# Adding the experts' returned rows by accumulating DMAs, and moving seven p @ ple_proj steps into the first expert pair

## The chip, the cores and the metric

The kernel runs on one core of a Trainium2 chip. The metric is the device time of one execution in microseconds; the median of three runs is given. A further execution was recorded by the hardware profiler, and all rows of the trace come from that one.

## The reference

One decoder layer over 512 tokens of width 1024, in float32. Three head groups (gated linear attention, stick-breaking attention, pooling) are mixed and added to x; call the sum h. Then comes a mixture of experts: for each token one of four groups, and two of the eight experts in it. Then a gated per-layer embedding, and a last norm:

```python
h = h + mix @ w_out
t = rmsnorm(h, norm2_g)                    # routed: top-1 group, top-2 experts of 32
y = sum over the two experts e of combine[e] * (silu(t @ w_gate[e]) * (t @ w_up[e])) @ w_down[e]
h = h + y
gate = sigmoid(rmsnorm(h, ple_norm_g) @ ple_gate_w + ple_gate_b)
h = h + gate * (p @ ple_proj_w)
return rmsnorm(h, final_norm_g)
```

## The kernel before

Tokens lie in four tiles of 128 (t = 0 to 3), kept in SBUF as h1[t], 128 x 1024. After the mixers `ffn` runs three stages.

Routing. For each tile `route_in` transposes the two halves of h1[t] on TensorE, copies them out on ScalarE (L759) and sums the squares there (L761); `logits` multiplies the halves by the router's matrix (L766); `route` is a generator of small VectorE steps, which first scales the tile's rows and writes them to a table in DRAM (tnd, L776) and then finds the group and the two experts (L780 to L813); `position` counts each expert's tokens before the tile (L820, L821), which gives a slot for each token. `one_hot` and `slot_sums` turn this into a list of tokens for a pair of experts, and `fetch` (L917) gathers their rows from tnd by an indirect DMA on Pool into xg. In the last part of this stage `ple(n)` issues the next n of sixteen steps of p @ ple_proj_w (L718, copied out by L720 into eo); step by step they are spread between the routing of tiles 2 and 3 by the tuple PLE, and fifteen stand ahead of gather_T(0, 0) and one behind it. PE and SP run in the order in which the program is written, VectorE too in this block.

Experts. Sixteen pairs (i = 0 to 15) run one after the other. `gather_T` transposes the pair's token rows (L941, scaled into xT by L942), `gate_up` multiplies them by the gate and up matrices in eight steps k with two experts each (L953), `down` by the down matrix (L985). Behind each k the function made by `between(i)` prepares a later pair. The result of a pair goes by an indirect DMA on Pool (L998) to its tokens' rows of yd in DRAM, which has one block of 512 rows for the first expert and one for the second. Pair 15 alone doesn't go through yd: `scatter` adds it by a matmul with a one-hot (L1006) and a VectorE add into h1 (L1008).

Weights come as 1 MB slabs, six a pair, by `load_units` on SP (L689). Slots are handed round in a ring: `free` puts a slot at its end, `load_units` loads into each slot that the ring has, and waits for the slot's last reader. Each load also waits for the load three before it (AHEAD). Slabs are taken in the order 0, 3, 1, 4, 2, 5 of a pair: the first two are used by k = 0 to 3 of `gate_up`, the next two by k = 4 to 7, the last two by `down`. The matrix ple_proj_w (pW) holds one slot of the ring, freed ahead of the first pair.

Tail. From pair 14 on VectorE and ScalarE too run in the written order. On SP stand the loads of ple_gate_w (`gate_load`, four of 1 MB), two rows and the four reads of yd (`load_y`, both returns of a tile in 1 MB). `add_y(t)` adds the two returns to h1[t] on VectorE (L1090). `split_gate(k)` splits a row block of the gate matrix into two parts (ScalarE L1019, VectorE L1022). `turn(t, hf)` transposes h1[t] (L1140) and splits it, `last(t)` multiplies it by the gate matrix (L1161) and `finish` makes the output. The adds and scatter of tile t + 1 stand in the middle of tile t's products.

Of the kernel before, what the change touches and what calls it, by code (L numbers as in the profile page):

```python
# [17 lines left out]
P = 128  # L18
S = 512
# [10 lines left out]
PLE = (2, 1, 2, 3, 1, 2)  # L30
# [581 lines left out]
def ffn(ctx, tc, A, K, mixh, mixl, out, dbg, stage):  # L612
# [99 lines left out]
    def ple_steps():  # L712

        for j in range(8):
            t, hf = j // 2, j % 2
            p = ps("pe", "pe")
            for k in range(2):
                PE.matmul(p, pT[:, k * S + t * P:k * S + (t + 1) * P], pW[:, k, hf * 512:hf * 512 + 512], start=(k == 0), stop=(k == 1))  # L718
                if k:
                    e = SC.activation(eo[t // 2][:, t % 2, hf * 512:hf * 512 + 512], p, AF.Copy)  # L720
                yield e if k else None
# [27 lines left out]
    def route_in(t, hf):  # L749

        if hf == 0:
            rt_in[t] = small("ms2", 2), {}, ps("pl", "po")
        ms2, hT, pl = rt_in[t]
        hs = slice(hf * 512, hf * 512 + 512)
        p = zt("xt")
        for k in range(4):
            PE.transpose(p[:, k * P:(k + 1) * P], h1[t][:, (4 * hf + k) * P:(4 * hf + k + 1) * P], ident)
        hT[hf] = xt_half(hf)
        SC.activation(hT[hf].rearrange("p k n -> p (k n)"), p, AF.Copy)  # L759
        junk = mw.tile([P, 512], BF, name="junk", tag="hidT")  # L760
        SC.activation(junk, h1[t][:, hs], AF.Square, accum_out=ms2[:, hf:hf + 1])  # L761
# [62 lines left out]
    def weights(t, g8, e8, id2, c0):  # L824
# [7 lines left out]
        SC.activation(ed, d, AF.Exp)  # L832
# [192 lines left out]
    with tc.manual_schedule(engines={mybir.EngineType.DVE}):  # L1025
        position(1)
        steps = [route(t) for t in (NT - 2, NT - 1)]
        run(steps[0], 7)
        ple(PLE[0])
        logits(NT - 1, 0)  # L1030
        ple(PLE[1])
        logits(NT - 1, 1)
        for t in (0, 1):
            one_hot(0, t)
        load_units(1)
        while run(steps[0], 1):
            run(steps[1], 1)
        ple(PLE[2])
# [3 lines left out]
        ple(PLE[3])  # L1042
        one_hot(0, 2)
        position(NT - 1)
        ple(PLE[4])
# [5 lines left out]
        ple(PLE[5])  # L1051
# [6 lines left out]
    ple(15 - sum(PLE))  # L1058
    for hf in range(2):
        gather_T(0, hf)  # L1060
    done = ple(1)
    with tc.issue_after(done.ins):
        SC.preload_act_table_set("silu_and_others")
    free(pW)
# [4 lines left out]
    def between(i):  # L1069

        def go(k):
            if k == (0 if i else 3) and i + 2 < 16:
                slots_of(i + 2)
            if k == 4 and i < 2:
                for t in range(NT):
                    one_hot(i, t)
            if k == (2 if i > 1 else 6):
                slot_weights(i)
            if k == 5 and i + 1 < 16:
                gather_T(i + 1, 0)  # L1080
            if i == 15 and k == 5:
                onehot_T(i)
        return go

    ys = []

    def add_y(t):

        for r in range(2):
            V.tensor_tensor(h1[t], h1[t], ys[t][:, r], ALU.add)  # L1090

    def load_y(t):
        ys.append(unit(F32, [P, 2, D]))
        nc.sync.dma_start(ys[t], yd.rearrange("(r n) d -> n r d", r=2)[t * P:(t + 1) * P])

    ends = ExitStack()
    for i in range(16):
# [3 lines left out]
        free(*(slab[6 * i + n] for n in (0, 3, 1, 4)))  # L1101
        if i == 15:
            break
# [5 lines left out]
        if i == 14:  # L1109
            gate_load(0)  # L1110
            load_y(0)
            for j in range(1, 4):
                gate_load(j)
            rows = mix.tile([P, 2, D], F32, name="rows", tag="m0")
            nc.sync.dma_start(rows[:, 0], bcast(A["ple_gate_b"]))
            for t in range(1, NT):
                load_y(t)
# [16 lines left out]
    def turn(t, hf):  # L1134

        if hf == 0:
            hT[t] = unit(F32R, [P, 2, D], slot_of[id(ys[t])][0])
# [63 lines left out]
    def sums(t):  # L1201
        add_y(t)
        for hf in range(2):
            scatter(2 * t + hf)
# [7 lines left out]
    def behind_down(n):  # L1212
        if n == 0:
            add_y(0)
        if n == 1:
            split_gate(0)
# [4 lines left out]
    split_gate(1)  # L1221
# [180 lines left out]
```

## Time and profile before

| | us |
|---|---|
| median of 3 runs | 562.84 |
| lowest, highest | 561.83, 564.35 |
| the profiled execution | 564.24 |
| its span, first to last instruction | 562.5 |
| TensorE busy (share of the span) | 515.2 (92%) |
| VectorE busy | 274.3 (49%) |
| ScalarE busy | 210.2 (37%) |
| Pool busy | 88.2 (16%) |

The span falls into the mixers (to about 197 us), the out projection with the routing (to about 249 us), the expert pairs (to about 484 us) and the tail. Busy shares are averages over stages with different limits. The profile's page gives the transfers' busy share in 40 equal slices of 14.06 us; queue q1 is that of SP, q0 the software queue of Pool. A chain of waits follows the last instruction back, at each step to what released it.

### The profile page before, as it was taken

How to read it: one execution, taken by the hardware profiler on the slowest of the kernel's cores; microseconds unless marked ns; L12 is line 12 of the kernel's file. 1: busy time of each engine (PE TensorE's matmuls, PEld its weight loads, DVE VectorE, ACT ScalarE, POOL GpSimd, SP SyncE). 2: the span in 40 equal slices, each digit the busy share in tenths (PEclk: the TensorE clock that was granted, in tenths of full speed). 3: DMA queues.
4: the chain of work that ended last, by engine and by line, in shares of the span. 5: the costliest groups of instructions: out<-in, count | busy, mean ns of one | idle time of the engine just before them, and what ended most of it. 6: DMA issues, size and time to landing. Idle time of an engine off the chain costs nothing.

```text
span 562.5 us, 7377 instructions
## 1 busy us (share of the span) xinstructions
PE 515.2 (92%) x2629; PEld 311.8 (55%) x2629; DVE 274.3 (49%) x729; ACT 210.2 (37%) x435; POOL 88.2 (16%) x125
## 2 busy tenths in 40 slices
PE   8999999999999999999999999998889888678992
PEld 5798886877997788743333333332322323247782
DVE  6662957756746664674422222222212101597774
ACT  7466665746757444441111111111111011364442
POOL 3300111221009400121111111111100100010000
PEclk9899999999999999999999999999999999899997
DMA  8882222300439669769999999999999999960111
GB/s 312 269 314 59 56 76 70 89 26 2 130 131 420 245 264 419 282 222 372 395 416 413 392 392 373 363 408 388 403 418 421 416 395 421 410 257 37 38 38 43
DMA packets 35787, 148.98 MB, mean 265 GB/s; under 512 B 6665, under 2 KB 13705, under 8 KB 22306
## 3 DMA queue, kind: packets, MB, share of 16 engines
q1 hardware_dynamic: 30562, 139.29, 64.2%
q0 software_dynamic: 4464, 8.11, 3.9%
q10 hardware_dynamic: 720, 1.05, 0.5%
q8 instruction: 23, 0.38, 0.3%
q14 instruction: 18, 0.15, 0.1%
HBM read 140.14 MB, written 16.25 MB: 278 GB/s over the span
## 4 chain that ended last, share of the span: by engine, by line
PE 62%; DMA 20%; DVE 8%; ACT 6%; issue 2%; POOL 1%; SPq 0%; DVEq 0%; ACTq 0%; POOLq 0%
DMA unit<-in_w_exp_dram 16%; PE gu L953 11%; PE pj L232 9%; PE po L78 8%; PE dn L985 6%; PE pj L255 5%; PE z L255 4%; PE pg L1161 3%; PE pe L718 2%; PE z L309 2%; PE po L331 2%; DMA yd<-big,idy 2%; DVE h L1090 2%; PE pl L766 1%; PE xt L941 1%
## 5 line engine op out<-in xcount | busy, mean ns | idle before, releaser
L953 PE MATMUL gu<-unit,xT 128*64 128x512 f32 x512 | 129.8, 601 | 6.2 <-DMA unit<-in_w_exp_dram 6.2
L953 PEld LDWEIGHTS gu<-unit,xT 128*64 128x64 f32 x512 | 36.5, 136 | 71.9 <-issue 55.4
L985 PE MATMUL dn<-unit,hidT 128*64 128x512 f32 x256 | 59.1, 598 | 7.6 <-ACT hidT L976 7.6
L942 DVE TENSOR_TENSOR xT<-xt,g2c 128x512 f32<-128x512 f32 x32 | 22.0, 688 | 66.4 <-PE xt L941 66.4
L958 ACT ACTIVATE sg<-gu 128x256 f32<-128x256 f32 x16 | 6.1, 384 | 126.0 <-PE gu L953 126.0
L232 PE MATMUL pj<-xh,wp 128*128 128x512 f32 x176 | 52.1, 403 | 0.2 <-ACT wp L67 0.2
L1161 PE MATMUL pg<-unit 128*128 128x512 f32 (+1 forms) x216 | 48.2, 378 | 1.2 <-DVE unit L1022 1.2
L1161 PEld LDWEIGHTS pg<-unit 128*128 128x128 f32 x216 | 37.2, 191 | 10.5 <-DVE unit L1022 3.2
L998 POOL DMA_INDIRECT yd<-big,idy x15 | 15.1, 1009 | 173.3 <-ACT big L989 173.3
L985 PEld LDWEIGHTS dn<-unit,hidT 128*64 128x64 f32 x256 | 18.1, 136 | 37.9 <-issue 25.3
L904 DVE COPY SL<-sl 128x10 f32<-128x10 f32 (+1 forms) x18 | 3.0, 168 | 72.7 <-PE sl L903 72.7
L232 PEld LDWEIGHTS pj<-xh,wp 128*128 128x128 f32 x176 | 33.2, 192 | 8.3 <-ACT wp L67 1.1
L989 ACT ACTIVATE big<-dn 128x512 f32<-128x512 f32 x30 | 17.9, 597 | 48.2 <-PE dn L985 48.2
L68 DVE TENSOR_TENSOR wp<-wraw,wp 128x768 fp32r<-128x768 f32 (+2 forms) x28 | 25.8, 928 | 15.3 <-ACT wp L67 15.1
L67 ACT ACTIVATE wp<-wraw 128x768 fp32r<-128x768 f32 (+2 forms) x28 | 22.8, 816 | 21.9 <-PE pj L232 9.8
L232 PE MATMUL pj<-xl,wp 128*128 128x512 f32 x88 | 30.0, 408 | 0.0
L941 PEld LDWEIGHTS xt<-ident,xg 128*128 128x128 f32 x128 | 13.5, 140 | 24.9 <-issue 24.6
L78 PE MATMUL po<-wo,mx 128*128 128x512 f32 x96 | 25.7, 408 | 0.0
L255 PE MATMUL pj<-wp,xh 128*128 128x384 f32 x96 | 24.8, 351 | 0.0
L78 PE MATMUL po<-unit,mx 128*128 128x512 f32 x96 | 23.8, 399 | 0.0
L941 PE MATMUL xt<-ident,xg 128*128 128x128 f32 x128 | 20.7, 286 | 0.0
L917 POOL DMA_INDIRECT xg<-tnd,idx x16 | 16.4, 1027 | 23.0 <-issue 13.1
(293 smaller groups left out, 847.5 us busy)
## 6 DMA issues: line engine op xcount, KB each, us to landing
unit<-in_w_exp_dram SPq DMA_DIRECT2D x96, 1024.0 KB, 8.3
wraw<-in_w_in_dram SPq DMA_DIRECT2D x20, 384.0 KB, 3.5
yd<-zero SPq DMA_DIRECT2D x4, 1024.0 KB, 8.6
unit<-in_ple_gate_w_dram SPq DMA_DIRECT2D x4, 1024.0 KB, 11.0
unit<-yd SPq DMA_DIRECT2D x4, 1024.0 KB, 16.1
wraw<-in_w_out_dram SPq DMA_DIRECT2D x8, 256.0 KB, 3.0
h<-in_x_dram SPq DMA_DIRECT2D x4, 512.0 KB, 5.3
unit<-in_w_out_dram SPq DMA_DIRECT2D x4, 512.0 KB, 9.6
```

The costliest lines, as they stand in the source:

```text
L67: nc.scalar.activation(h, src, AF.Copy)
L68: nc.vector.tensor_tensor(l, src, h.bitcast(F32), ALU.subtract)
L78: nc.tensor.matmul(p, a[k][:, ts_], K["wo"][k][:, b, hs], start=(n == 0), stop=(n == 3 * len(ks) - 1))
L232: PE.matmul(q, a[:, i * P:(i + 1) * P], b[k], start=(n == 0), stop=(n == 3 * KC - 1))
L255: PE.matmul(p[t][:, :W_IN[j]], a[k][:, t * P:(t + 1) * P], b, start=(n == 0), stop=(n == 3 * KC - 1))
L917: G.indirect_dma_start(out=xg[i % 2], out_offset=None, in_=tnd, in_offset=bass.IndirectOffsetOnAxis(ap=idx[:, i:i + 1], axis=0), bounds_ch ...
L941: PE.transpose(p[:, k * P:(k + 1) * P], xg[i % 2][:, (4 * hf + k) * P:(4 * hf + k + 1) * P], ident)
L942: V.tensor_tensor(xTs[i, hf], p.rearrange("p (a b) -> p a b", a=4), g2c[:, 4 * hf:4 * hf + 4, None].to_broadcast([P, 4, P]), ALU.mult)
L953: PE.matmul(gu[64 * e:64 * e + 64], xTs[i, k // 4][:, k % 4, 64 * e:64 * e + 64], w[e][k // 4][:, 512 * (k % 4):512 * (k % 4) + 512], star ...
L985: PE.matmul(dn[64 * e:64 * e + 64], hT[:, f, 64 * e:64 * e + 64], w[e][2][:, 1024 * f + 512 * hf:1024 * f + 512 * hf + 512], start=(f == 0 ...
L989: SC.activation(o[:, 512 * hf:512 * hf + 512], dn, AF.Copy)
L1161: PE.matmul(p, hT[t][:, a, ks], gw[k][:, b, hs], start=start and n == 0, stop=stop and n == len(ab) - 1)
```

## The change

The four reads of yd and the eight VectorE adds go. In their place eight DMAs on Pool's queue, issued behind pair 14, add the rows of yd to h1 in SBUF: the first expert's returns of all four tiles, then the second's. The four loads of the gate matrix stand together on SP. hT takes its slots from the ring. Behind the down products of pair 15, split_gate(1) moves ahead of the scatters.

In the routing block, tile 3's logits come ahead of all but one step of p @ ple_proj; tile 2's steps run through ahead of most of tile 3's; nine ple steps stand ahead of the first gather_T and seven go between the k steps of gate_up(0), the last eight products in the banks "sc". pW is freed behind gate_up(0). The load of the Silu table moves behind the last Exp. In `route_in` the sum of squares is queued behind the copy on ScalarE.

```diff
-            p = ps("pe", "pe")
+            p = ps("pe", "pe" if j < 4 else "sc")
...
-        SC.activation(hT[hf].rearrange("p k n -> p (k n)"), p, AF.Copy)
+        turned = SC.activation(hT[hf].rearrange("p k n -> p (k n)"), p, AF.Copy)
         junk = mw.tile([P, 512], BF, name="junk", tag="hidT")
-        SC.activation(junk, h1[t][:, hs], AF.Square, accum_out=ms2[:, hf:hf + 1])
+        with tc.issue_after(turned.ins):
+            SC.activation(junk, h1[t][:, hs], AF.Square, accum_out=ms2[:, hf:hf + 1])
...
-        run(steps[0], 7)
-        ple(PLE[0])
         logits(NT - 1, 0)
-        ple(PLE[1])
+        ple(1)
         logits(NT - 1, 1)
+        run(steps[0], 9)
+        run(steps[1], 1)
+        run(steps[0])
         for t in (0, 1):
             one_hot(0, t)
         load_units(1)
-        while run(steps[0], 1):
-            run(steps[1], 1)
-        ple(PLE[2])
+        ple(1)
         position(NT - 2)
         run(steps[1])
         load_units(1)
-        ple(PLE[3])
+        ple(2)
         one_hot(0, 2)
         position(NT - 1)
-        ple(PLE[4])
+        ple(1)
         one_hot(0, 3)
         fetch(0)
         G.memset(xg[1], 0.0)
         for t in range(NT):
             one_hot(1, t)
-        ple(PLE[5])
+        ple(2)
         fetch(1)
...
-    ple(15 - sum(PLE))
+    with tc.issue_after(K["exp"].ins):
+        SC.preload_act_table_set("silu_and_others")
+    ple(2)
     for hf in range(2):
         gather_T(0, hf)
-    done = ple(1)
-    with tc.issue_after(done.ins):
-        SC.preload_act_table_set("silu_and_others")
-    free(pW)
...
         def go(k):
+            if i == 0 and k < 7:
+                ple(1)
...
-    def add_y(t):
+    def add_y():
 
         for r in range(2):
-            V.tensor_tensor(h1[t], h1[t], ys[t][:, r], ALU.add)
-
-    def load_y(t):
-        ys.append(unit(F32, [P, 2, D]))
-        nc.sync.dma_start(ys[t], yd.rearrange("(r n) d -> n r d", r=2)[t * P:(t + 1) * P])
+            for t in range(NT):
+                G.dma_start(h1[t], yd[r * S + t * P:r * S + (t + 1) * P], accum_op=ALU.add)
...
         free(*(slab[6 * i + n] for n in (0, 3, 1, 4)))
+        if i == 0:
+            free(pW)
...
         if i == 14:
-            gate_load(0)
-            load_y(0)
-            for j in range(1, 4):
+            add_y()
+            for j in range(4):
                 gate_load(j)
             rows = mix.tile([P, 2, D], F32, name="rows", tag="m0")
             nc.sync.dma_start(rows[:, 0], bcast(A["ple_gate_b"]))
-            for t in range(1, NT):
-                load_y(t)
...
-            hT[t] = unit(F32R, [P, 2, D], slot_of[id(ys[t])][0])
+            hT[t] = unit(F32R, [P, 2, D], hT_slots[t])
...
     def sums(t):
-        add_y(t)
         for hf in range(2):
             scatter(2 * t + hf)
...
-        if n == 0:
-            add_y(0)
-        if n == 1:
-            split_gate(0)
+        if n < 2:
+            split_gate(n)
 
     down(15, behind_down)
     for hf in range(2):
         scatter(hf)
-    split_gate(1)
+    hT_slots = ring[6:10]
+    del ring[6:10]
```

## Rows read from the trace of the kernel before

**Rows 1.** The page: busy share of the DMA engines in 40 slices, in tenths

```profile
DMA  8882222300439669769999999999999999960111
```

**Rows 2.** Chain of waits that ended last: start us, us, what

```profile
450.87 7.88 DMA unit<-in_w_exp_dram
...
469.73 8.48 DMA yd<-big,idy
...
478.28 6.17 DMA unit<-yd
```

**Rows 3.** Waits of the SP queue, whole span: us in total, times, longest us

```profile
SPq L689 <- DMA unit<-in_w_exp_dram: 199.0, 81, 8.6
...
SPq L689 <- PE pe L718: 4.0, 1, 4.0
```

**Rows 4.** Busy time by stretch; the last three columns: PEclk, DMA share, GB/s

```profile
248.00:256.00 8.00, 7.70 (x39) 2.61 (x39) 6.09 (x32) 1.88 (x2) 0.99 (x1) 1.00 0.68 227
256.00:264.00 8.00, 6.90 (x36) 2.33 (x34) 3.15 (x13) 1.52 (x4) 0.00 (x0) 1.00 1.01 417
264.00:470.00 206.00, 186.69 (x875) 64.83 (x873) 47.12 (x194) 27.91 (x57) 27.64 (x28) 1.00 1.00 399
```

**Rows 5.** Tail: timeline of VectorE's adds; TensorE's waits from 490 us on

```profile
484.47 2.49 DVE L1090 TENSOR_TENSOR h<-h,unit 128x1024 f32<-128x1024 f32 x2 [5.48 <-DMA unit<-yd]
...
489.27 0.68 DVE L1008 TENSOR_TENSOR h<-h,sc 128x512 f32<-128x512 f32 x1
...
501.73 2.48 DVE L1090 TENSOR_TENSOR h<-h,unit 128x1024 f32<-128x1024 f32 x2
...
PE xt L1140 <- DVE h L1008: 5.3, 3, 2.5
```

**Rows 6.** Timeline of routing and first pair: start us, us, engine, line, operation [idle before]

```profile
226.13 0.22 DVE L780 SCALAR_TENSOR_TENSOR gp<-pl,rs,rb 128x4 f32<-128x4 f32 x1 [0.20 <-PE pl L766]
...
228.94 0.25 DVE L813 SCALAR_TENSOR_TENSOR Ab<-io,id,c 128x32 bf16<-128x32 f32 x1
...
231.83 1.88 PE L718 MATMUL pe<-unit,big 128*128 128x512 f32 x4
...
232.73 0.22 DVE L780 SCALAR_TENSOR_TENSOR gp<-pl,rs,rb 128x4 f32<-128x4 f32 x1 [0.72 <-POOL rs L61]
...
236.38 0.22 DVE L780 SCALAR_TENSOR_TENSOR gp<-pl,rs,rb 128x4 f32<-128x4 f32 x1 [1.32 <-PE pl L766]
...
240.10 0.25 DVE L813 SCALAR_TENSOR_TENSOR Ab<-io,id,c 128x32 bf16<-128x32 f32 x1
...
241.85 0.95 POOL L1048 MEMSET xg<- 128x1024 f32 x1 [6.18 <-DMA tnd<-xg]
...
243.19 1.24 POOL L917 DMA_INDIRECT xg<-tnd,idx  x1 [0.39 <-DVE Dm L910]
...
247.21 1.04 PE L941 MATMUL xt<-ident,xg 128*128 128x128 f32 x8
...
249.04 3.65 PE L953 MATMUL gu<-unit,xT 128*64 128x512 f32 x16
...
256.91 1.08 PE L953 MATMUL gu<-unit,xT 128*64 128x512 f32 x4
```

**Rows 7.** DMA issues near 241, 249 and 471.4 us, with us to landing; SP timeline

```profile
xg<-tnd,idx POOLq DMA_INDIRECT x1, 3.6
...
unit<-in_w_exp_dram SPq DMA_DIRECT2D x1, 1024.0 KB, 4.9
...
unit<-in_w_exp_dram SPq DMA_DIRECT2D x1, 1024.0 KB, 8.0
...
471.77 0.43 SPq L1015 DMA_DIRECT2D unit<-in_ple_gate_w_dram  x1
```

**Rows 8.** Pool's scatter; packets, MB, share by queue in 473.5:474.0, then 474.0:475.5

```profile
469.73 0.98 POOL L998 DMA_INDIRECT yd<-big,idy  x1 [15.80 <-ACT big L989]
...
q0 software_dynamic: 1, 0.00, 2.0%
...
q1 hardware_dynamic: 63, 0.43, 68.9%
q0 software_dynamic: 64, 0.20, 33.1%
```

More of the change, by code (lines that the diff above doesn't have):

```diff
@@ L29 @@
 FILL = (8, 3, 0, 1, 0, 1, 0, 1, 0, 1, 1, 1, 4, 2, 2, 2, 9)
-PLE = (2, 1, 2, 3, 1, 2)
 AHEAD = 3
@@ L831, in weights @@
         SC.activation(ge, gp[:, t, :4], AF.Exp, bias=ngm, accum_out=gsum)
-        SC.activation(ed, d, AF.Exp)
+        K["exp"] = SC.activation(ed, d, AF.Exp)
         yield
@@ L1083, in between @@
         return go
-    ys = []
-    def add_y(t):
+    def add_y():
         for r in range(2):
-            V.tensor_tensor(h1[t], h1[t], ys[t][:, r], ALU.add)
-    def load_y(t):
-        ys.append(unit(F32, [P, 2, D]))
-        nc.sync.dma_start(ys[t], yd.rearrange("(r n) d -> n r d", r=2)[t * P:(t + 1) * P])
+            for t in range(NT):
+                G.dma_start(h1[t], yd[r * S + t * P:r * S + (t + 1) * P], accum_op=ALU.add)
     ends = ExitStack()
```

## The prediction

> **What bounds the kernel now.** Read the page's slice of DMA shares first [rows 1]: the transfers are full from about 250 us to about 495 us, and outside that stretch they aren't. The chain of waits that ended last says the same [rows 2]: its later expert pieces are transfers of expert weights, then the scatter of pair 14, then the first read of the returned rows. The SP queue says what the loads wait for [rows 3]: 199 us in 81 waits on the load three before it, so on transfers, and one 4.0 us wait on L718, the release of the slot of `pW`. The sums by stretch give the rate [rows 4]: share 0.68 and 227 GB/s in 248 to 256, then 1.01 and 417 GB/s, and 1.00 over 206 us. So from about 256 us each weight arrives when the stream gets to it. TensorE is 90% busy there but waits for the stream at the end. **A microsecond in which the transfers idle before 256 us is a microsecond at the end; TensorE time saved there counts only through the slots that it frees.** Behind the stream comes the tail, where TensorE waits for VectorE's adds, 5.3 us in three waits [rows 5].
>
> **Part 1, the routing and the first pair.** Sixteen steps of p @ ple_proj are two matmuls each; two of them took 1.88 us [rows 6], 0.94 us a step. Before, fifteen stand ahead of the first gather_T and one behind it. After, nine stand ahead of it and seven in the first pair. Taken from the path ahead of the gather: 6 x 0.94 = 5.6 us of TensorE.
>
> How much of that comes out earlier? The routing chain decides. Tile 3's logits lose two of the steps ahead of them, 1.9 us, and VectorE loses its 1.32 us wait for them [rows 6]. But VectorE used to run the two tiles' steps interleaved and now runs them nearly one after the other. Tile 1's own chain, from L780 at 226.13 to the end of L813 at 229.19, took 3.06 us [rows 6]. Two such chains from 232.73 on, with 0.35 for the mean square of tile 3, 0.5 for two one_hots and 0.2 for a position between them, end near 239.8, against 240.35 (L813 at 240.10 plus 0.25). That is 0.55 gained. One step of ple instead of its queue of three then stands ahead of position(3), 0.3 more. The list of slots comes near 241.7. The memset of xg[1] waited until 241.85 for the write of tile 3's row copy, after which the gather went out at 243.19 [rows 6]. After, that write is issued ahead of two 1 MB loads instead of behind one, so it no longer holds Pool. I put the gather at 242.1, its landing 3.6 us later [rows 7] at 245.7, gather_T there instead of at 247.21, and gate_up(0) at 247.4 instead of 249.04: the chain gives 1.6 of the 5.6 us. The other 4 us are TensorE standing still, in front of 6.6 us (7 x 0.94) that it now does inside the pair. The moved table load comes ahead of the last copies of eo and can hold the PSUM bank that gate_up(0) takes; 0.3 of the 247.4 is for that. The squares put behind the copies move each by at most 0.63 us, ahead of a VectorE that gets to them later; I cost them at nothing.
>
> Now the slots. Before, `pW` was freed ahead of the pair, and its load went out near 249.1. The slots of the first two weight slabs came free with the sixteenth matmul of gate_up(0), at 249.04 + 3.65 = 252.7, those of the next two at 256.91 + 1.08 = 258.0 [rows 6]. After, the first two come at 247.4 + 3.65 + 3 x 0.94 = 253.9, and the other two, and `pW` with them, at 247.4 + (258.0 - 249.04) + 6.6 = 263.0, or 262.7 if a step fills the 0.3 us gap. So two loads (2.1 MB, 5 us at 417 GB/s) stand between 253.9 and 262.7, and the stream is idle for the rest. An isolated load takes 4.9 us to land [rows 7] where its bytes take 2.5, so bytes flow about 1 us after issue, at 263.6. Until 263.6 the stream before had moved 8 x 0.227 + 7.6 x 0.417 = 5.0 MB [rows 4]; after it has moved two loads and a gather, 2.4 MB. The missing 2.6 MB are **6 us** at 417 GB/s, and a full stream gives nothing back. Bounds: if the chain came as early as TensorE allows (gate_up(0) 5.6 us earlier, at 243.4) the slots come at 259.0 and the loss is about 2; if the chain gained nothing, 7.5. What would hide the loss is slack in the stream later; [rows 4] shows none.
>
> **Part 2, the returned rows.** Removed: four reads of 1 MB on SP, and eight adds of 1.24 us on VectorE. Two of them (2.49 us) stood ahead of the first scatter add at 489.27; the pairs in the three later tiles stood ahead of the transposes, and TensorE's 5.3 us of waits there [rows 5] go. Next is TensorE itself in these tiles, so the 5.3 us are taken whole.
>
> Added: eight accumulating transfers of 0.52 MB on Pool's queue. The trace has no accumulating transfer and no plain one on this queue; the nearest rows are the scatters and gathers on it. h1[0] is whole with the fifth of the eight, after 2.62 MB, since all first returns go ahead of all second ones. On SP, the gate loads no longer wait behind the read that waited for the scatter: 5.2 MB (four gate loads, two rows) are issued from 471.8 on and are in front when the scatter lands at 478.2. With the end of the last weight load (471.4 + 8.0 [rows 7]) 5.7 MB are queued there.
>
> The scatter of pair 14 was on Pool at 469.73 and its first packet was seen only in the window from 473.5 [rows 8], about 4.2 us. So the first accumulating bytes flow at 478.3 + 4.2 = 482.5, and SP's queue has 5.7 - 4.2 x 0.417 = 3.95 MB left. Beside a full SP queue the software queue got 0.20 MB in 1.5 us, SP's 0.43 MB [rows 8]: 0.13 and 0.29 MB/us; I take 0.12 and 0.30. SP's part ends at 482.5 + 13.2 = 495.7; the other queue has moved 1.6 MB by then, and the last 1.0 MB take 2.5 us alone, 498.2, with 0.8 for the landing 499. The second round waits for the first round's landing, but by the same rate the queue still has three others then.
>
> h1[0] at 499 instead of the scatter add's start at 489.27 delays that add by 9.7 us. Behind it in the hand-written order of ScalarE and VectorE stand the copies of turn(0) and all gate splits from k = 2 on, so nothing is done in the meantime. **9.7 - 5.3 = +4.4 us.** The later tiles come 0.5 MB apart, ahead of their need. Bounds: all of the software queue first, 482.5 + 2.62/0.417 + 0.8 = 489.6, which gives -5.0; an accumulating byte at twice the engine time, should the old value cost as much as the new, so 0.06 MB/us beside SP, 0.21 alone: 0.8 MB by 495.7, the other 1.8 MB 8.7 us, 505.2, which gives +10.6. I take the plain price, since only transfers without an add have rows.
>
> The Trainium skill, DMA: Bandwidth & Descriptors, "Queues, rings and completion order", says that each DMA engine goes round its queues packet by packet; with packets of one size that is the even share among the rivals below, +1.2 for this part. The rows show about a third for the software queue, so here the measurement decides.
>
> **The sum.** 6.0 + 4.4 = +10.4 on the profiled execution's own 564.24 us (span 562.5), 574.6. That execution lies 1.4 above the median of 562.84; on the median it is **573.2 us**.
>
> **Rivals.** *Not slower: the software queue goes first.* If the accumulating transfers pass the gate loads, part 2 is -5.0 and the sum +1.0: 563.8. For it speaks only that the rows are those of scatters and gathers, not of plain transfers; against it the third that the trace shows. It decides when h1[0] lands before about 490. With part 1 at its low end of 2 the sum is -3.0, 559.8: the one faster case. *The accumulate costs double.* 6.0 + 10.6 = +16.6, 579.4; no row speaks for or against it. *The routing chain shrinks to what TensorE allows.* Part 1 is 2, the sum +6.4, 569.2; against it speak the VectorE chain and the 3.6 us landing. *Even shares.* If the software queue moves half of 0.417, 0.21 MB/us, beside SP, h1[0] comes at 495.8, part 2 is +1.2 and the sum +7.2: 570.0; the third in [rows 8] speaks against it. The Trainium skill's rule on the queues, cited above, would give this case. That the change doesn't do what it says could be if the adds stayed serial on Pool: each second add waiting for a landing behind a full queue, 4.2 us each [rows 8]; three such exposed add 12.6 us, 586, beyond my high end.
>
> **How the numbers follow.** Forecast 0.45, even shares 0.15, chain shorter 0.10, double price 0.12, serial 0.03, the software queue first 0.11 with part 1 at 6 and 0.04 with part 1 at 2. Each spreads by a few us, as its bounds do; the range 563 to 580 leaves out about 2 in 10. Faster or slower by 0.5%, 2.8 us, is about what a measurement of this kernel tells from no change: faster (under 560.0) 0.06, the last of these cases and the low edge of others; within 0.5% 0.13, mostly the software queue first; slower 0.81.
>
> **What would show it.** Right: transfers under half full between 246 and 253 and idle again near 259 to 263; gate_up(0) from about 247.4 with its end near 263; the last weight wait near 479 instead of 473; TensorE idle between the first scatter product and a scatter add some 20 us behind the scatter's landing; no wait on the adds in the three later tiles. Wrong: the stream full from 254 on, or the first scatter add within 12 us of that landing.

## The result, and the profile after

The changed kernel takes 583.01 us (median of 4 runs, 582.51 to 585.34) against 562.98 us before: 1.036 times as long, 95% interval 1.0327 to 1.0399, some 20 us more. The forecast said 573.2 us, in a range from 563 to 580. Its direction was right, its size was half of what came. The profiled execution, whose rows follow, is the slowest of the four (585.34 us, span 583.6).

The page of the kernel after, its DMA slices to be held against [rows 1]: the dip in the middle (8, 5, 3, 8) lies where the kernel before had 9, 7, 6, 9, and TensorE's clock has a new dip there and another near the end.

```profile
PEclk9899999999999999799999999999999989569997
DMA  9871222300479488538999999999999999970111
```

Busy time by stretch of the kernel after; the last three columns are granted clock, DMA share and GB/s, as in [rows 4]:

```profile
248.00:256.00 8.00, 6.45 (x25) 2.29 (x26) 6.36 (x32) 2.69 (x9) 0.76 (x1) 1.00 0.18 51
256.00:264.00 8.00, 8.00 (x30) 2.51 (x31) 1.59 (x9) 1.19 (x2) 0.99 (x1) 1.00 0.59 230
264.00:272.00 8.00, 6.90 (x36) 2.46 (x34) 2.99 (x13) 1.96 (x4) 0.00 (x0) 1.00 0.67 247
272.00:470.00 198.00, 178.29 (x832) 60.40 (x828) 44.85 (x186) 26.11 (x53) 27.40 (x27) 1.00 1.00 399
```

In 248 to 256 the transfers move 51 GB/s where they moved 227, in 256 to 264 230 instead of 417. From 272 on the stream is as full as before (399 GB/s) and gives nothing back. That is the forecast's mechanism for the first part, at almost twice its size: the first part alone, timed below, costs 11.8 us where 6.0 were forecast.

Timeline of TensorE in the kernel after (start, us, instruction, idle before), and the stretch with the lowest clock:

```profile
231.57 0.64 PE L756 MATMUL xt<-ident,h 128*128 128x128 f32 x4
233.48 1.05 PE L766 MATMUL pl<-rw,xT 128*128 128x36 f32 x8 [1.27 <-ACT junk L761]
...
236.90 2.05 PE L717 MATMUL pe<-unit,big 128*128 128x512 f32 x2
...
243.00 1.10 PE L717 MATMUL pe<-unit,big 128*128 128x512 f32 x2
...
249.14 1.09 PE L941 MATMUL xt<-ident,xg 128*128 128x128 f32 x8 [1.22 <-DMA xg<-tnd,idx]
250.65 1.08 PE L953 MATMUL gu<-unit,xT 128*64 128x512 f32 x4 [0.41 <-issue]
251.66 1.13 PE L717 MATMUL pe<-unit,big 128*128 128x512 f32 x2
...
265.70 1.08 PE L953 MATMUL gu<-unit,xT 128*64 128x512 f32 x4
```

```profile
236.00:238.00 2.00, 2.00 (x8) 1.48 (x8) 0.49 (x3) 1.02 (x1) 0.00 (x0) 0.50 0.37 147
```

TensorE stops for 1.27 us ahead of the last tile's logits, and soon after runs at 0.50 of its clock (1.2 GHz): the two matmuls of a step take 2.05 us there and 1.10 at full clock. The gather goes out at 245.46 (243.19 in [rows 6]), gate_up(0) starts at 250.65 (249.04) and ends at 266.8 (258.0); the kernel before has the figures in brackets. The next rows are the gather and scatter on Pool with its accumulating transfers (h<-yd), then the first load of SP after the routing:

```profile
245.46 1.30 POOL L917 DMA_INDIRECT xg<-tnd,idx  x1 [4.39 <-DVE Dm L910]
...
482.89 0.98 POOL L998 DMA_INDIRECT yd<-big,idy  x1 [17.95 <-ACT big L989]
491.05 3.70 POOL L1088 DMA_DIRECT2D h<-yd  x4 [7.17 <-DMA yd<-big,idy]
501.36 0.86 POOL L1088 DMA_DIRECT2D h<-yd  x1 [6.62 <-DMA h<-yd]
```

```profile
257.94 16.52 SPq L688 DMA_DIRECT2D unit<-in_w_exp_dram  x7
```

In the tail VectorE's first scatter add waits 17.5 us for the accumulating transfers, and starts at 515.88; before, it stood at 489.27 [rows 5]. TensorE waits once behind it, and the three waits in the later tiles, 5.3 us in all, are gone:

```profile
515.88 1.28 DVE L1008 TENSOR_TENSOR h<-h,sc 128x512 f32<-128x512 f32 x2 [17.51 <-DMA h<-yd]
```

```profile
PE xt L1133 <- DVE h L1008: 17.4, 1, 17.4
```

The scatter of pair 14 landed at 490.75, so that add came 25.1 us behind the landing, against 489.27 - 478.21 = 11.1 before. The first part cost 490.75 - 478.21 = 12.5 us of this execution and the second 25.1 - 11.1 - 5.3 = 8.7, together 21.2, the difference of the spans (21.1).

### The profile page after: what moved, and what is told of

The parts are those of the page before. It is cut to its first block, busy times and chain, and to the rows that moved or that the text cites. A ratio compares the mean times of both kernels' runs of the same rounds, so it can differ in the third digit from the quotient of the medians.

```text
span 583.6 us, 7387 instructions
## 1 busy us (share of the span) xinstructions
PE 522.0 (89%) x2629; PEld 312.5 (54%) x2629; DVE 266.4 (46%) x721; ACT 210.1 (36%) x435; POOL 94.7 (16%) x133
## 3 DMA queue, kind: packets, MB, share of 16 engines
q10 hardware_dynamic: 720, 1.05, 0.5%
## 4 chain that ended last, share of the span: by engine, by line
PE 69%; DMA 17%; issue 6%; DVE 4%; ACT 2%; POOL 1%; SPq 0%; ACTq 0%; POOLq 0%; DVEq 0%
PE gu L953 13%; PE pj L231 9%; PE po L77 8%; DMA unit<-in_w_exp_dram 7%; PE pg L1154 7%; PE dn L985 7%; PE pj L254 5%; DMA yd<-big,idy 4%; PE z L254 4%; DMA h<-yd 2%; PE z L308 2%; PE pe L717 2%; PE po L330 2%; PE pl L766 1%; PE xt L941 1%
## 5 line engine op out<-in xcount | busy, mean ns | idle before, releaser
L953 PE MATMUL gu<-unit,xT 128*64 128x512 f32 x512 | 132.0, 605 | 7.6 <-DMA unit<-in_w_exp_dram 7.1
L985 PEld LDWEIGHTS dn<-unit,hidT 128*64 128x64 f32 x256 | 17.4, 136 | 38.7 <-issue 27.1
L67 DVE TENSOR_TENSOR wp<-wraw,wp 128x768 fp32r<-128x768 f32 (+2 forms) x28 | 25.8, 928 | 15.2 <-ACT wp L66 15.0
L66 ACT ACTIVATE wp<-wraw 128x768 fp32r<-128x768 f32 (+2 forms) x28 | 22.8, 816 | 21.8 <-PE pj L231 10.6
## 6 DMA issues: line engine op xcount, KB each, us to landing
h<-yd POOLq DMA_DIRECT2D x8, 512.0 KB, 13.2
```

Of the source, the lines that this page charges most:

```text
L66: nc.scalar.activation(h, src, AF.Copy)
L67: nc.vector.tensor_tensor(l, src, h.bitcast(F32), ALU.subtract)
L953: PE.matmul(gu[64 * e:64 * e + 64], xTs[i, k // 4][:, k % 4, 64 * e:64 * e + 64], w[e][k // 4][:, 512 * (k % 4):512 * (k % 4) + 512], star ...
L985: PE.matmul(dn[64 * e:64 * e + 64], hT[:, f, 64 * e:64 * e + 64], w[e][2][:, 1024 * f + 512 * hf:1024 * f + 512 * hf + 512], start=(f == 0 ...
```

## The experiments

Each was timed against runs of the kernel before on the same chip; a ratio is given with its 95% interval in brackets, and is turned into microseconds with 563. Single executions differ by 2 to 3 us in when the work ahead of the routing ends, so stages are told from one mark, the start of the last transposes of tile 3's rows (231.35 before, 231.57 in the row above). All in us after the mark, read from the timelines of Pool, TensorE and SP; the last column is the measured difference. The forecast's row is its own times less 231.35; its down(0) is put 2.1 us behind its end of gate and up (262.7 to 263.0), as in the kernel before:

| kernel | gather issued | gate_up(0) starts | first load of SP | down(0) starts | scatter of pair 14 | time against before |
|---|---|---|---|---|---|---|
| before | 11.8 | 17.7 | 17.8 | 28.8 | 238.4 | |
| forecast, part 1 | 10.8 | 16.1 | 22.6 | 33.6 | +6.0 | +6.0 |
| late_slot | 11.8 | 17.7 | 21.4 | 28.8 | 241.1 | +2.8 |
| routing_all_ahead | 13.2 | 23.0 | 21.8 | 33.6 | 243.0 | +5.0 |
| moved_only | 11.6 | 17.1 | 25.0 | 36.0 | 247.9 | +11.0 |
| routing_bank | 10.5 | 18.5 | 26.6 | 37.5 | 248.6 | +9.7 |
| routing_warm | 10.4 | 16.9 | 25.8 | 36.8 | 248.6 | +11.1 |
| routing_only | 12.6 | 18.4 | 27.1 | 38.1 | 248.8 | +11.8 |
| after (both parts) | 13.9 | 19.1 | 26.4 | 37.3 | 251.3 | +20.4 |

The theory at the start was that the two parts add, and that each was mis-sized by a step of its own; the rivals were that they meet in one place, and for the first part that the stop and the half clock, not the slots, are the loss.

### The two parts alone

**routing_only**: the first part, with the tail of before (the edit against the changed kernel).

```
-            add_y()
-            for j in range(4):
-                gate_load(j)
+            gate_load(0)
+            load_y(0)
+            for j in range(1, 4):
+                gate_load(j)
...
```

> The first part of the change alone: new order of the routing block, seven steps in the first pair, late release of pW, squares behind copies; the tail is that of the kernel before. Theory (the two parts add up; in the changed kernel the scatter of pair 14 landed at 490.75 us against 478.21, 12.5 later): +11 to +13 us, 574 to 576, stream idle from about 250 to 258 us and a granted clock of 0.5 for some 7 us from 235 us on. Rival (the first part costs what was forecast, 6, and the rest of the 12.5 comes from the tail's transfers or from chance): +5 to +7, 568 to 570.

576.07 us, 1.0209 of before (1.0173 to 1.0246), +11.8. **accum_only**: the second part, with the routing of before.

```
+        for r in range(2):
+            for t in range(NT):
+                G.dma_start(h1[t], yd[r * S + t * P:r * S + (t + 1) * P], accum_op=ALU.add)
...
-        add_y(t)
```

> The second part alone: accumulating transfers on Pool's queue in place of the reads and the VectorE adds; routing and first pair are those of the kernel before. Theory (an accumulating byte takes twice the engine time): the first scatter add starts about 25 us behind the landing of pair 14's scatter instead of 11, and 5.3 us of waits in later tiles go: +8 to +10, 571 to 573. Rival (plain price): the add 20 to 21 us behind the landing, +4 to +5, 567 to 568.

572.15 us, 1.0151 (1.0113 to 1.0190), +8.5. 2.09% and 1.51% make 3.60%; the change has 3.63%. The parts add, and can be looked at one by one.

### Part 1: the slots, or the stop and the clock

**late_slot**: the kernel before, with the slot of `pW` given back behind the first pair's gate and up.

```
-    free(pW)
...
+        if i == 0:
+            free(pW)
```

> The kernel before with one edit: the slot of p @ ple_proj's weights is given back behind the first pair's gate and up, as in the change, with all fifteen steps left where they were. It prices the stream's missing load by itself. If the stream of expert weights sets the time, one load of 1 MB that can't start near 249 but only near 258 is missing at the rate of a full stream (1 MB at 0.40 MB per us): +2.5 us, 567 us, with the DMA share of 248 to 256 down from 0.68 to about 0.3 and nothing else moved. If a later pair makes up for it, or the slot's load is hidden, no change: 564.6 within 0.5%. If the whole 9 us from 249 to 258 are lost, +6 or more: 571.

566.44 us, 1.0049 (1.0022 to 1.0076), +2.8, with nothing else moved: one missing load of 1.05 MB at 0.40 MB/us makes 2.6. The stream gave nothing back, and missing bytes were missing time.

**routing_warm**: routing_only with nine matmuls without use ahead of tile 3's logits, so that TensorE doesn't stop there.

```
+        hot = zt("hot")
+        for _ in range(9):
+            PE.matmul(hot[:, :384], ones, cm.rearrange("p a b -> p (a b)"), start=True, stop=True)
         logits(NT - 1, 0)
```

> As routing_only, with nine small matmuls of constants ahead of tile 3's logits, into a bank that nobody reads, so that TensorE isn't idle in the 1.3 us in which those logits wait. Theory (the idle stretch at 232.2 to 233.5 brings the clock to one half from 235 to 242 us, and that delays position and gather by about 3.5 us): clock 1.0 throughout, gather_T near 246, 3 to 4 us faster than routing_only: 570 to 572. Rival (the half clock hides behind VectorE's chain; the loss is the moved work and the slots): within 1 us of routing_only.

574.81 us, 1.0197 (1.0142 to 1.0253), +11.1. The clock in 232 to 242 was 1.00 instead of 0.83 and the gather went out at 242.90 instead of 244.63, but its transposes came 5.0 us behind that instead of 4.4 (the mark itself lies up to 1 us later here, behind six of the nine). Timeline of TensorE in routing_warm:

```profile
247.90 1.09 PE L941 MATMUL xt<-ident,xg 128*128 128x128 f32 x8 [2.54 <-DMA xg<-tnd,idx]
249.39 1.98 PE L953 MATMUL gu<-unit,xT 128*64 128x512 f32 x4 [0.40 <-issue]
```

Behind the wait for the gather the clock fell again (four matmuls took 1.98 us, 1.97 in routing_only, where the change has 1.08), and down(0) started at 269.26 instead of 270.15. The clock at the logits explains at most 1 us of the 11 (11.8 became 11.1), not the 3 to 4 of the theory that took it for the loss.

**routing_bank**: routing_only with tile 3's logits in a PSUM bank of their own.

```
-            rt_in[t] = small("ms2", 2), {}, ps("pl", "po")
+            rt_in[t] = small("ms2", 2), {}, ps("pl", "po" if t < NT - 1 else "p3")
```

> The change's first part alone, as in routing_only (576.07 us, 1.021 of before), with one edit: the last tile's logits are written to a PSUM bank of their own. It asks what TensorE's 1.27 us stop at 232 to 233.5 waits for. If it waits for VectorE to have read tile 2's logits out of the one bank, the stop goes (below 0.3 us), the granted clock of 232 to 242 stays at 0.95 or more (0.83 in routing_only), the gather is issued near 243 (244.63), and the time falls by about 1 us only, as routing_warm showed for the clock: 574 to 576. If it waits for ScalarE's copy and squares of the last tile, the stop stays above 1 us and nothing moves: 576, gather at 244.6.

572.98 us, 1.0172 (1.0135 to 1.0209), +9.7. The stop is gone: in routing_bank's timeline the logits follow without idle time.

```profile
229.88 0.98 PE L766 MATMUL pl<-rw,xT 128*128 128x36 f32 x8
```

So the stop came from sharing the bank with tile 2's logits, which VectorE still had to read, not from ScalarE's `junk` that the profile names. In the change VectorE's last read of them ends at 233.33 and the matmuls start at 233.48:

```profile
233.09 0.24 DVE L781 SCALAR_TENSOR_TENSOR lg<-pl,rs,rb 128x32 f32<-128x32 f32 x1
```

Of the time only about 2 us came back, again because the gather (issued 10.5 after the mark, the forecast's 10.8) took 6.1 us to its transposes.

**routing_all_ahead**: the new order of the routing, all sixteen steps ahead of the first pair.

```
-    ple(2)
+    ple(9)
     for hf in range(2):
         gather_T(0, hf)
+    free(pW)
```

> The change's first part with its new order of the routing (logits ahead), but all seven moved steps back in front of the first pair's turned tokens, and the slot given back there. It separates the order from the moved steps. If the moved steps and the late slots are the loss: the seven steps lie in the wait for the gathered tokens (some 7 us at 1.0 us each, of the 6 us or so between the last routing operation and the landing), the first pair starts near 250 and ends near 259, the stretch 256 to 264 is full again (above 0.9), and the time is 1 to 3 us above before: 566 to 568. If the order alone delays the chain (stop at 232, half clock, gather later), most of the 11.4 us stays: 572 or more.

568.95 us, 1.0088 (1.0058 to 1.0117), +5.0: between the two expectations. The order does cost, but less through the stop, with which the gather goes out 1.4 us later, than through the steps: gate_up(0) starts 5.3 us later. Nine steps now stand between the routing and the first gather_T, where four stood before; of the five more, four had stood in gaps of the routing and one behind gather_T. The gather landed 3.9 us after its issue at 242.91, so TensorE works through the last of them with the tokens already there. Its timeline in the kernel before, then in routing_all_ahead:

```profile
243.70 3.68 PE L718 MATMUL pe<-unit,big 128*128 128x512 f32 x8
```

```profile
243.42 7.97 PE L717 MATMUL pe<-unit,big 128*128 128x512 f32 x18
251.23 1.04 PE L941 MATMUL xt<-ident,xg 128*128 128x128 f32 x8
```

**moved_only**: the old order, seven steps moved into the first pair.

```
-PLE = (2, 1, 2, 3, 1, 2)
+PLE = (2, 1, 2, 2, 1, 1)
...
+            if i == 0 and k < 7:
+                ple(1)
```

> The kernel before with its own order of the routing, seven of the sixteen steps of p @ ple_proj moved into the first pair, and their weights' slot given back behind it (with the table load and the bank that this needs). Beside routing_all_ahead (the new order alone, +5.0 us) it completes the square of the change's first part (+11 us). If the two add up, the moved steps cost 11.4 - 5.0 = +6.4 us, 570. The forecast's own working for moved steps says the same by another way, +6.0, if gate and up of the first pair run from about 247.4 to 262.7: this run tests the working of the slots without the new order's stop and half clock. If the steps are slower inside the pair than 0.94 us each (1.06 in the trace of the change), the end is near 264 and the time 571. If moved steps are harmless in the old order, 565 to 567.

574.56 us, 1.0196 (1.0156 to 1.0236), +11.0: more than every expectation. With the old order, without the stop ahead of the logits, the moved steps cost nearly what the whole first part costs (9.5 of 10.4 us at the scatter of pair 14). Timeline of TensorE in moved_only, then SP's first load:

```profile
244.49 1.97 PE L941 MATMUL xt<-ident,xg 128*128 128x128 f32 x8 [3.49 <-DMA xg<-tnd,idx]
246.43 1.67 PE L953 MATMUL gu<-unit,xT 128*64 128x512 f32 x4
...
262.07 1.08 PE L953 MATMUL gu<-unit,xT 128*64 128x512 f32 x4
```

```profile
254.31 19.09 SPq L689 DMA_DIRECT2D unit<-in_w_exp_dram  x8
```

TensorE had 3.49 us with nothing to do, ahead of seven steps of which some could have filled them. It came out at half clock (transposes 1.97 us instead of 1.04), the pair started 0.6 us earlier after the mark than before, and its down(0) 7.2 later. The order on top of it changes little (+0.9 at the scatter): by itself it costs because steps stand behind the routing, and with the moved steps these are gone.

**act_order**: the kernel before, the squares behind the copies.

```
+        turned = SC.activation(hT[hf].rearrange("p k n -> p (k n)"), p, AF.Copy)
...
+        with tc.issue_after(turned.ins):
```

> The kernel before with ScalarE's squares put behind the copies of the turned tokens, alone. Costed at nothing in the forecast: no change, 564 within 0.5%. If the squares then end too late for the logits' scale, VectorE waits up to 0.63 us for each of the last two tiles and the gather goes out about 1 us later: 565 to 566.

564.40 us, 1.0005 (0.9986 to 1.0023): nothing, as costed.

### Part 2: the byte's price, or the place in line

**plain_on_pool**: the returned rows read by plain transfers on Pool's queue in the change's order, the adds left on VectorE.

```
-        nc.sync.dma_start(ys[t], yd.rearrange("(r n) d -> n r d", r=2)[t * P:(t + 1) * P])
+        for r in range(2):
+            for t in range(NT):
+                G.dma_start(ys[t][:, r], yd[r * S + t * P:r * S + (t + 1) * P])
```

> The tail of the kernel before with the returned rows read by eight plain transfers of 0.5 MB on Pool's queue, in the same order as the accumulating ones and with the four gate loads ahead on SP; VectorE adds them as before. Nothing is accumulated by a transfer. Theory (the add doubles a byte's price): alone the software queue moves about 0.4 MB/us instead of 0.21, the first VectorE add starts about 19 to 21 us behind the scatter's landing: +12 to +15 us in all, since the later adds stay (575 to 578) while the eight transfers are done by about 502. Rival (the place in the queue and the sharing, not the add): 0.21 MB/us alone too, the fifth landing 25 us behind, +18 to +20, 581 to 583.

575.21 us, 1.0189 (1.0133 to 1.0245). The place in line is the change's, the byte is plain. Packets, MB and share of 16 engines by queue in plain_on_pool, 486 to 490 (beside SP) and 498 to 500 (alone), then VectorE's second add of tile 0:

```profile
q1 hardware_dynamic: 158, 1.15, 69.6%
q0 software_dynamic: 148, 0.51, 32.3%
...
q0 software_dynamic: 227, 0.81, 101.7%
```

```profile
499.33 1.23 DVE L1090 TENSOR_TENSOR h<-h,unit 128x1024 f32<-128x1024 f32 x1 [10.36 <-DMA unit<-yd]
```

The plain queue has 0.13 MB/us beside SP's 0.29 and 0.40 alone, and tile 0 is there 20.5 us after the first transfer was issued (478.87), 21 behind the scatter's landing (478.3): the forecast's 0.12, 0.30 and 20.8. The same view of accumulating transfers, kernel after, 498 to 500 beside SP, then of accum_only in 503 to 505, alone:

```profile
q1 hardware_dynamic: 59, 0.43, 53.0%
q0 software_dynamic: 55, 0.21, 52.3%
```

```profile
q0 software_dynamic: 115, 0.43, 107.4%
```

Alone, 0.21 MB/us: half of the plain rate, with the engines full. Beside SP the queue keeps 0.105 MB/us, since it takes half of the engines' time instead of a third. The first figure of each row, the packets, says why. Beside each other the two queues move nearly packet for packet: 63 and 64 in [rows 8], 158 and 148 with plain rows, 59 and 55 with accumulating ones. A packet of the software queue held an engine for 0.14 us plain and 0.30 accumulating, beside SP or alone, and one of SP's for 0.28 to 0.29 (worked out from the rows: share times stretch times 16, by packets). So tile 0 is whole 25 to 26 us behind the landing. The Trainium skill, DMA: Bandwidth & Descriptors, "Rules for kernel authors", says that an accumulating DMA reads its destination and writes it later; the halved rate agrees with two reads for each byte written.

**accum_pairs**: accum_only with the order (tile 0, 1), (tile 2, 3).

```
-        for r in range(2):
-            for t in range(NT):
+        for t0 in (0, 2):
+            for r in range(2):
+                for t in (t0, t0 + 1):
```

> accum_only (572.15 us) with the eight accumulating transfers in another order: both returned rows of tiles 0 and 1, then those of tiles 2 and 3, so that the first tile is whole with the third transfer and not with the fifth. If the price is the bytes in front (double engine time, 0.12 MB per us beside SP's queue), the third goes out when the first has landed, near 485, and lands at 491 to 494; the first scatter add comes some 8 us earlier than in accum_only (502.2) and the time is 564 to 567. If each accumulating transfer takes its 10 us from issue to landing whatever is in front, the third lands at 496 and the time is 568 to 570. If the place in line does nothing, 572.

572.93 us, 1.0164 (1.0124 to 1.0203). It says nothing on the question, since the new order didn't come about. Pool issues four transfers in a row, as in accum_only; a tile's second return waits for its first, so these are the first returns of all four tiles:

```profile
475.37 3.70 POOL L1090 DMA_DIRECT2D h<-yd  x4 [7.03 <-DMA yd<-big,idy]
```

It is a repetition of that kernel (+8.5 and +9.2). **accum_in_line** fixes the order on Pool:

```
+        with tc.manual_schedule(engines={mybir.EngineType.Pool}):
             for t0 in (0, 2):
```

> accum_only (572.15 us) with the eight accumulating transfers in the order that accum_pairs was meant to have, now held on Pool's queue by hand (in accum_pairs the scheduler had put the four first returns in front again, the order of accum_only): rows 1 and 2 of tiles 0 and 1, then those of tiles 2 and 3. If the price is the bytes in front at 0.12 MB per us, the third transfer goes out near 485, when the first has landed, and lands near 494; the first scatter add comes there instead of at 502.2 and the time is 564 to 567. If an accumulating transfer takes its 10 us and more whatever is in front, the third lands at 496 to 498 and the time is 567 to 570. If the place in line does nothing, 572.

565.55 us, 1.0027 (1.0003 to 1.0050), +1.5. Pool's accumulating transfers, then VectorE's first scatter add:

```profile
477.61 1.91 POOL L1091 DMA_DIRECT2D h<-yd  x2 [8.26 <-DMA yd<-big,idy]
487.88 0.86 POOL L1091 DMA_DIRECT2D h<-yd  x1 [8.36 <-DMA h<-yd]
...
496.55 1.28 DVE L1008 TENSOR_TENSOR h<-h,sc 128x512 f32<-128x512 f32 x2 [10.94 <-DMA h<-yd]
```

The add comes 19 us behind the landing instead of 26: the place in line was worth 7 us of the 8.5. Still, each of the two transfers of tile 0 took 8.7 to 10.3 us from issue to landing with at most one other transfer of their queue beside them, so the shorter line doesn't bring back the 11 us of the kernel before.

### Is the gain in the later tiles to be had?

**pool_adds**: the reads of before, the adds of tiles 1 to 3 on GpSimd.

```
-            V.tensor_tensor(h1[t], h1[t], ys[t][:, r], ALU.add)
+            (G if t else V).tensor_tensor(h1[t], h1[t], ys[t][:, r], ALU.add)
```

> The kernel before with the adds of the returned rows of tiles 1 to 3 on GpSimd in place of VectorE; the reads stay as they are on SP's queue. It asks whether the 5.3 us that the change won at these waits can be had without accumulating DMAs. If VectorE's order is what makes the three tiles late (h waited on for 5.3, 3 and 2.5 us together with the adds), the waits fall and the time is 559 to 563. If GpSimd's add of 128 x 1024 takes more than twice VectorE's, TensorE waits for it as long or longer: 564 to 570.

566.15 us, 1.0053 (1.0028 to 1.0079), +3.0: in the second expectation's range, but by another way than it said. Timeline of Pool in pool_adds, then VectorE's in the kernel before and in pool_adds:

```profile
495.04 9.86 POOL L1090 TENSOR_TENSOR h<-h,unit 128x1024 f32<-128x1024 f32 x3 [25.95 <-DMA unit<-yd]
```

```profile
493.80 7.26 DVE L1022 SCALAR_TENSOR_TENSOR unit<-unit,g3c 128x1024 fp32r<-128x1024 f32 x6 [0.34 <-ACT unit L1019]
```

```profile
492.36 13.62 DVE L1022 SCALAR_TENSOR_TENSOR unit<-unit,g3c 128x1024 fp32r<-128x1024 f32 x6 [0.36 <-ACT unit L1019]
```

Beside GpSimd's adds VectorE's six gate splits took 13.62 us; in the kernel before the same six took 7.26. TensorE's waits moved from the adds (5.3 us) to the gate weights that come of these splits (6.3 us). The Trainium skill, SBUF — State Buffer, "SBUF: two separate sides", says that a VectorE operation with two SBUF inputs and a GpSimd operation that reads SBUF lock each other out; the 6.4 us more agree with it.

**accum_rest**: tile 0 as before, accumulating transfers for tiles 1 to 3 only.

```
+        if t == 0:
+            nc.sync.dma_start(ys[t], yd.rearrange("(r n) d -> n r d", r=2)[t * P:(t + 1) * P])
+    def add_rest():
+        for r in range(2):
+            for t in range(1, NT):
+                G.dma_start(h1[t], yd[r * S + t * P:r * S + (t + 1) * P], accum_op=ALU.add)
```

> The kernel before with tile 0 as it was (one read on SP's queue, adds on VectorE) and the returned rows of tiles 1 to 3 alone added by six accumulating transfers. It asks whether the 5.3 us of waits in the later tiles can be had without a late first tile. If tile 0's rows still land as before, the first scatter add is near 489 and the time falls by up to 5 us: 559 to 561. If the accumulating transfers take half of the engines' time from the gate load and the read of tile 0 (2.1 MB at some 0.22 in place of 0.40 MB per us), the first scatter add is 3 to 4 us late and the sum is -2 to 0: 562.5 to 564.5. If the gate weights come too late for tile 0's products, 567 or more.

563.78 us, 1.0011 (0.9982 to 1.0041): no difference, as the middle expectation had it. VectorE's adds of tile 0 wait 9.17 us for their read, where [rows 5] has 5.48, so of the 5.3 us won in the later tiles about 4 are lost here:

```profile
486.39 2.48 DVE L1090 TENSOR_TENSOR h<-h,unit 128x1024 f32<-128x1024 f32 x2 [9.17 <-DMA unit<-yd]
```

**accum_late**: the same, the accumulating transfers held on Pool until tile 0's read has landed, tile 1 first.

```
+        with tc.manual_schedule(engines={mybir.EngineType.Pool}):
+            G.tensor_copy(small("seen", 1), ys[0][:, 1, D - 1:])
+            for r, t in ((0, 1), (0, 2), (1, 1), (0, 3), (1, 2), (1, 3)):
```

> accum_rest (563.78 us, 1.001 of before) with the six accumulating transfers of tiles 1 to 3 held back on Pool until tile 0's read has landed, tile 1's two first. In accum_rest tile 0's read landed 10 us after the scatter instead of 6, which ate the 5.3 us that fell away in the later tiles. If that is all, the first scatter add returns to 11 us behind the scatter's landing and the time falls to 559 to 561. If tile 1's second transfer (which waits for the landing of its first, some 10 us each) then lands later than 24 us behind the scatter's landing, where tile 1 needs it, the gain is lost there: 562 to 566.

**559.32 us, 0.9924 of before (0.9896 to 0.9953): faster than both kernels.** Pool's transfers, VectorE's first scatter add, and TensorE's wait for the adds in accum_late:

```profile
481.98 1.24 POOL L1099 COPY seen<-unit 128x1 f32<-128x1 f32 x1 [13.79 <-DMA unit<-yd]
483.17 1.90 POOL L1101 DMA_DIRECT2D h<-yd  x2
493.44 1.76 POOL L1101 DMA_DIRECT2D h<-yd  x2 [8.37 <-DMA h<-yd]
```

```profile
486.74 0.68 DVE L1008 TENSOR_TENSOR h<-h,sc 128x512 f32<-128x512 f32 x1
```

```profile
PE xt L1148 <- DVE h L1008: 0.8, 1, 0.8
```

SP's read of tile 0 went out at 475.42, with the scatter's landing; 486.74 is 11.3 us behind it, as before, and of the 5.3 us of waits 0.8 is left: 4.5 gained, 4.3 measured.

## Why the prediction was wrong

**Right.** What bounds the kernel (the stream from 256 us on, then the tail's first tile); that a missing byte is missing time (late_slot, +2.8 for one load); that the two parts add; the removal of 5.3 us in the later tiles (accum_late, -4.3); the squares at nothing; the plain price of a byte on the software queue. Of the signs named in the forecast these came: a stream under half full in 246 to 253 (share 0.25), nearly idle again (0.14 in 266 to 268, some 6 us later than forecast), no waits on the adds in later tiles.

**Wrong in part 1: the start of gate_up(0), and the pair's own length.** The step that failed is "the chain gives 1.6 of the 5.6 us". Measured from the mark, the forecast put the start at 16.1; no kernel got there. In the old order the chain gave 0.6 (moved_only, 17.1), and in the change it lost 1.4 (19.1). Its VectorE work didn't end earlier in the old order (gather at 11.6); a stop for a PSUM bank and half clock were added in the new one (13.9). Where the gather did go out at 10.4 or 10.5, near the forecast's 10.8, it took 5 to 6 us, with two loads issued 4 to 5 us ahead of it, instead of the 3.6 of [rows 7]. The pair itself was costed at 0.94 us a step; it took 1.06 and, in several runs, began at half clock, so gate and up took 16.1 us in the change and 16.7 in moved_only, for 15.6.

Both errors push the slots, and with them the time from which the stream is full again. Against the forecast down(0) is 2.4 us late in moved_only, 4.5 in routing_only and 3.7 in the change, and the first load by as much. Each of these microseconds is lost beside the forecast's 6.0: 8.4, 10.5 and 9.7, where the scatter of pair 14 came 9.5, 10.4 and 12.9 late. So the term was right in kind and too small through those two inputs. In moved_only about 1 us isn't assigned, in the one profiled execution of the change about 3. Of these 1.6 lie in pair 14, in TensorE's rows of the change, then of routing_only:

```profile
470.32 3.25 PE L953 MATMUL gu<-unit,xT 128*64 128x512 f32 x6 [2.04 <-DMA unit<-in_w_exp_dram]
473.50 0.98 PE L941 MATMUL xt<-ident,xg 128*128 128x128 f32 x4
```

```profile
469.88 1.93 PE L953 MATMUL gu<-unit,xT 128*64 128x512 f32 x6 [1.87 <-DMA unit<-in_w_exp_dram]
471.74 0.66 PE L941 MATMUL xt<-ident,xg 128*128 128x128 f32 x4
```

Behind the wait for weights the change ran at 0.50 of the clock in 472 to 474, routing_only at 1.00. The median of the change is 2.3 us below that execution, and the parts timed alone add up to 20.3 of that median's 20.4, so these microseconds need not be there in every execution.

That the stop and the half clock were the main loss would have been the easy story, since they are the most visible rows of the trace after. routing_warm and routing_bank remove the stop and win 0.7 and 2.1 us; moved_only never has it ahead of the logits and loses nearly as much (11.0 of 11.8). The seven steps are the loss: before, most of them stood in the wait for the gather and held gate_up(0) up by 0.6 us at most, in the pair they stand between the weights' arrival and the release of the slots that these hold.

**Wrong in part 2: the price of an accumulating byte.** The forecast had the double price as a rival (0.12) and took the plain one, "since only transfers without an add have rows". That choice is the second step that failed. The double price is what the runs show: 0.21 MB/us alone, as that rival said; beside SP 0.105, better than its 0.06, because the two queues take turns by packets and the slower packets so get half of the engines' time. The forecast read a third of the bytes in [rows 8] as speaking against equal turns; the same rows have 63 and 64 packets, and SP's are about twice as large. Its byte rates for plain rows held all the same. So h1[0] was whole 25.1 us behind the landing: the forecast had 20.8, the rival 27.0. plain_on_pool shows the chosen price right to 0.3 us for transfers that don't add (21 against 20.8). Part 2 is then 25.1 - 11.1 - 5.3 = +8.7, between the forecast's +4.4 and the rival's +10.6; accum_only alone measured +8.5.

The range failed because both errors went the same way: its top of 580 held the double price on an unchanged part 1, or a longer part 1 (bound 7.5) on the plain price, and 7.5 was too tight a bound, worked out for a chain that "gained nothing", not for one that loses.

## What to carry to other kernels

Work that is moved out of a wait still costs its whole length where it lands; first ask what it had been covering. Ahead of a stream that is full to its end, what counts of a stage is when it gives its buffers back: put no work that can stand elsewhere ahead of the last read that frees a buffer. Put a new kind of transfer behind the one that the next tile waits for and give it the tiles with time to spare: the accumulating transfers that cost 8.5 us for all tiles gain 4.3 for the last three.

## What the runs showed of the hardware

An accumulating DMA into SBUF moves its bytes at half the plain rate: 0.43 MB in 2 us at 107% of the engines, against 0.81 MB in 2 us at 102%. A queue's part beside another isn't a fixed share of bytes or of time: 32% of the time for plain rows, 52% for accumulating ones, with 0.13 and 0.105 MB/us. What stays is the count of packets, 148 beside 158 and 55 beside 59. TensorE's granted clock was 0.50 (1.2 GHz) in 236 to 238 of the change, a few us after a stop of 1.27 us at 232, and 1.00 there with the stop removed (routing_warm, routing_bank). Behind waits of 1.22 us at 248 in the change and 1.87 at 468 in routing_only it stayed at 1.00; soon after waits of 1.90 us at 247 in routing_only, 2.04 at 468 in the change and 3.49 in moved_only it was 0.50. GpSimd's three adds stretched six VectorE operations from 7.26 to 13.62 us.
